# A two-layer encoder trunk on one core: layer 1's attention prepared by key head, its output weights split a piece per step, and the router's sums in one matmul

## The chip, the cores and the metric

The kernel runs on one core of one Trainium2 chip. TensorE (PE) does the matmuls and transposes, VectorE (DVE), ScalarE (ACT) and GpSimd (POOL) the elementwise work, and SyncE (SP) issues the weight loads. The metric is the device time of one execution in microseconds (us), as the median of several runs. All times within an execution count from the start of its span.

## The reference

`reference()` applies two layers to x (512 tokens of 1024 features), all in float32. Each layer is a token mixer and then a mixture of experts, both post-norm and modulated by a conditioning vector:

```
mod = silu(c) @ ada_w[i] + ada_b[i];  sh1, sc1, g1, sh2, sc2, g2 = split(mod, 6)
h = x * (1 + sc1) + sh1
y = neighbourhood_mixer(h) if i == 0 else gqa_mixer(h)
x = layer_norm(ALPHA * x + (1 + g1) * y)
h = x * (1 + sc2) + sh2
y = hierarchical_moe(h)
x = layer_norm(ALPHA * x + (1 + g2) * y)
```

Layer 1's mixer has 16 query heads and 4 key heads of 64 features. Queries and keys are RMS-normalised and rotated (rope), scores are softmaxed over all 512 keys, and the result is multiplied by an output matrix of 1024 x 1024. The router of the experts picks, for each token, the best of 4 groups and the best 2 of its 8 experts, with gates from the two softmaxes. Each of the 32 experts is a gated MLP (1024 to 512 to 1024).

## The kernel before

Tokens lie on the 128 partitions, in 4 tiles t of 128 tokens. Where products need more than one pass's precision, an operand x is split into a rounded part H (ACT copies it to fp32r) and a rest L = x - H (a subtraction), and three matmuls H·H, H·L and L·H are added. `split()` (line 307) does this with the subtraction on POOL unless told otherwise.

The order of PE's instructions is the order of the program text. In layer 0's mixer the DVE keeps that order too, and SP does everywhere. On the other engines, and on the DVE elsewhere, a planner puts the instructions in order when the program is built: the text's order is the priority, and an instruction whose inputs are ready can go ahead of an earlier one that waits. Weights of 1 MB come through a fixed list (`plan`, `W`), each loaded into the next buffer that is free.

Layer 1's mixer is `mixer1` (line 717). It projects keys and values for all tokens (lines 751 to 763), then queries in four parts c, one for each key head (`project(c)`, 96 steps of one matmul). `ahead(c, x)` splits one half of the weights of part c; it is called for part c + 1 at the end of `project(c)`. `rope` rotates a projected tile and sums its squares; `root` makes the RMS factor. `keys(t)` scales the 4 key heads of tile t, splits them, and transposes H and L, each head laid twice side by side (8 transposes of 128 x 128), into kHL. `queries(c, t)` does the like for queries, with H and L side by side (4 transposes). The order is: project(0), then project(1) with keys(t) after each 12 steps, then queries(0, t) after each 12.

The attention then runs over 64 blocks n: part c = n // 16, tile t = n // 4 % 4, query head n % 4. `scores(n + 2)` makes 2 matmuls, a DVE maximum and an ACT exponential; `turn(n)` transposes the result of block n; `finish(u)` weighs the values of four blocks and splits the result (oH, oL; the latter on POOL). Between these, k steps of other PE work are filled in: 8 per block of project(2) and project(3) while c < 2, none for the first 3 blocks of each part and none for n < 36 once c is 2, else 5 steps of the output projection (`halves`, `sums`). At n = 24 `router_weights(1)` (line 389) folds the modulation into the router's weights: 8 matmuls against a broadcast column give a bias, and 8 more against ones give column sums, with a DVE multiplication between. At n = 32 `late()` (line 1099) splits all four 1 MB output weights in one go (`split_wo`, 16 pieces of 128 x 512: ACT copies, POOL subtracts in layer 1), then makes the gain g1 and the scaled norm rows gb by 6 row matmuls (`row`).

`sums(t, h, kh)` is 12 matmuls of the output projection for tile t, half h of the columns and half kh of the rows. For kh = 0 it also scales x by gb and adds to it, on the DVE. 192 steps in all; 125 are filled in before the last block. Then come, between the rest of the steps, `turnX` (transposes of x), `logits` (16 records of router matmuls and the norm's statistics) and `router` for tiles 0 to 2, and `split_z` (a POOL subtraction of 128 x 1024 for each tile).

`moe` (line 1367) is the same in both layers. `begin` gathers the first tokens from tiles 0 to 2 on PE, runs the router of tile 3, marks its slots (`mark`), and gathers tile 3. Then come 8 quarters q of 4 experts: `gate_up`, `turn`, `down`, `combine`. In q = 0 the work filled in behind `gate_up(0)` is gate2(0), gate2(1), the turn, counts, residual(0), residual(1). gate2 is a row matmul and a DVE copy of the second gain; residual(h) is 2 row matmuls and 8 DVE operations of 128 x 512, and holds both buffers `gc` until they are done. `counts` and `turn` share one buffer, `hx`.

## Time and profile before

| | |
|---|---|
| time, median of 3 runs | 1695.33 us (1695.08 to 1695.36) |
| time of the profiled execution | 1693.38 us |
| its span | 1691.6 us |
| mean granted TensorE clock | 0.964 |
| PE busy | 1572.1 us (93%) |
| DVE busy | 718.3 us (42%) |
| ACT busy | 447.8 us (26%) |
| POOL busy | 165.7 us (10%) |
| layer 0, mixer | about 0 to 350 us |
| layer 0, experts | about 360 to 862 us |
| layer 1, mixer | about 862 to 1160 us |
| layer 1, experts | about 1171 to 1665 us |

The profile lists one execution. A share of busy time is a mean over the whole span, so the two expert stages, 0.98 ms of the 1.69 ms, weigh most in it. A row of the timeline gives the start, the length, and behind the brackets how long the engine had been idle and what ended that. PE's rows overlap, since matmuls are pipelined. A granted clock of 1.00 is 2.4 GHz and 0.50 is 1.2 GHz; a value between them is a mean of the two levels over the stretch.

### The profile page before, as it was taken

How to read it: one execution, taken by the hardware profiler on the slowest of the kernel's cores; microseconds unless marked ns; L12 is line 12 of the kernel's file. 1: busy time of each engine (PE TensorE's matmuls, PEld its weight loads, DVE VectorE, ACT ScalarE, POOL GpSimd, SP SyncE). 2: the span in 40 equal slices, each digit the busy share in tenths (PEclk: the TensorE clock that was granted, in tenths of full speed). 3: DMA queues.
4: the chain of work that ended last, by engine and by line, in shares of the span. 5: the costliest groups of instructions: out<-in, count | busy, mean ns of one | idle time of the engine just before them, and what ended most of it. 6: DMA issues, size and time to landing. Idle time of an engine off the chain costs nothing. (4 is left out here: it accounts for less than half of the span.)

```text
span 1691.6 us, 21659 instructions
## 1 busy us (share of the span) xinstructions
PE 1572.1 (93%) x8618; PEld 923.7 (55%) x8618; DVE 718.3 (42%) x1616; ACT 447.8 (26%) x959; POOL 165.7 (10%) x107
## 2 busy tenths in 40 slices
PE   7999997989999999999978896997999999999995
PEld 5676664763445454444468774776354444545442
DVE  3434544664323232231367557667432232323235
ACT  2443334230111111111144655543111111111112
POOL 2322112110000000000032115002000000000001
PEclk9999997999999999999989898997999999999997
DMA  9577873159999999999731000026799999999981
GB/s 336 194 306 282 350 287 135 65 217 381 417 420 418 420 420 418 420 420 418 327 110 51 26 1 0 1 84 264 314 416 419 420 419 418 420 420 419 419 337 51
DMA packets 76199, 493.19 MB, mean 292 GB/s; under 512 B 9876, under 2 KB 11284, under 8 KB 18876
## 3 DMA queue, kind: packets, MB, share of 16 engines
q1 hardware_dynamic: 72636, 485.44, 70.4%
q10 hardware_dynamic: 3456, 6.29, 1.1%
q8 instruction: 70, 1.15, 0.3%
q14 instruction: 37, 0.30, 0.1%
HBM read 489.61 MB, written 2.10 MB: 291 GB/s over the span
## 5 line engine op out<-in xcount | busy, mean ns | idle before, releaser
L299 PE MATMUL gu<-w,xT 128*64 128x512 f32 x2048 | 445.0, 592 | 0.0
L299 PEld LDWEIGHTS gu<-w,xT 128*64 128x64 f32 x2048 | 146.9, 137 | 291.5 <-issue 288.1
L299 PE MATMUL pd<-w,hx 128*64 128x512 f32 x1024 | 227.1, 596 | 0.0
L1479 DVE TENSOR_TENSOR h<-h,gu 128x512 f32<-128x512 f32 x32 | 22.0, 687 | 370.5 <-PE gu L299 370.5
L299 PEld LDWEIGHTS pd<-w,hx 128*64 128x64 f32 x1024 | 70.8, 137 | 138.9 <-issue 135.6
L299 PE MATMUL gc<-OH,zH 128*128 128x256 f32 x480 | 123.5, 294 | 2.0 <-DVE OH L1364 2.0
L299 PE MATMUL gc<-OH,zL 128*128 128x256 f32 x480 | 120.4, 287 | 0.0
L299 PE MATMUL gc<-YH,OT 128*128 128x512 f32 x244 | 104.1, 427 | 1.0 <-DVE X L1446 1.0
L1446 DVE TENSOR_TENSOR X<-X,gc 128x512 f32<-128x512 f32 x128 | 87.2, 687 | 39.5 <-PE gc L299 39.5
L299 PEld LDWEIGHTS gc<-OH,zH 128*128 128x128 f32 x480 | 94.0, 196 | 13.5 <-issue 12.3
L299 PE MATMUL gc<-YL,OT 128*128 128x512 f32 x244 | 96.3, 395 | 0.0
L299 PEld LDWEIGHTS gc<-OH,zL 128*128 128x128 f32 x480 | 94.2, 196 | 0.0
L299 PE MATMUL pj<-w,oH 128*128 128x512 f32 x256 | 87.2, 409 | 0.7 <-DVE g L998 0.7
L1502 ACT ACTIVATE YH<-h 128x512 fp32r<-128x512 f32 x32 | 20.2, 630 | 231.0 <-DVE h L1501 231.0
L1382 ACT ACTIVATE xT<-gc,A 128x256 f32<-128x256 f32 x60 | 33.7, 564 | 175.0 <-PE gc L299 175.0
L299 PE MATMUL pj<-wh,hTH 128*128 128x256 f32 (+1 forms) x240 | 63.4, 312 | 9.4 <-DVE t L776 3.5
L299 PEld LDWEIGHTS gc<-YH,OT 128*128 128x128 f32 x244 | 45.8, 188 | 37.3 <-DVE X L1446 15.8
L1380 DVE TENSOR_SCALAR xT<-gc,A 128x256 f32<-128x256 f32 x60 | 32.5, 543 | 76.9 <-ACT xT L1382 76.5
L1478 ACT ACTIVATE h<-gu 128x512 f32<-128x512 f32 x32 | 19.1, 597 | 173.0 <-PE gu L299 173.0
L302 PE MATMUL pt<-c_ident,pr 128*128 128x128 f32 x384 | 61.6, 286 | 2.8 <-ACT pr L864 1.6
L299 PE MATMUL pj<-wl,hTH 128*128 128x256 f32 (+1 forms) x240 | 60.5, 301 | 2.0 <-POOL wl L312 2.0
L862 DVE TENSOR_REDUCE st<-ps 128x1 f32<-128x512 f32 x64 | 44.0, 689 | 38.5 <-PE ps L299 37.9
(331 smaller groups left out, 2440.2 us busy)
## 6 DMA issues: line engine op xcount, KB each, us to landing
w<-in_gu SPq DMA_DIRECT2D x256, 1024.0 KB, 14.3
w<-in_dn SPq DMA_DIRECT2D x128, 1024.0 KB, 13.9
w<-in_ada SPq DMA_DIRECT2D x40, 1024.0 KB, 7.3
wq<-in_wqk SPq DMA_DIRECT2D x16, 512.0 KB, 3.7
w<-in_wo SPq DMA_DIRECT2D x8, 1024.0 KB, 5.0
w<-in_adaq SPq DMA_DIRECT2D x6, 1024.0 KB, 11.5
bias<-in_nab ACTq DMA_DIRECT2D x24, 256.0 KB, 3.7
w<-in_wq SPq DMA_DIRECT2D x4, 1024.0 KB, 4.8
```

Of the source, the lines that this page charges most:

```text
L299: return self.nc.tensor.matmul(out, l, r, start=start, stop=stop, **kw)
L302: self.nc.tensor.transpose(out, in_, self.ident)
L862: nc.vector.tensor_reduce(s[:, 0:1], ps, axis=AX.X, op=OP.max, negate=True)
L1380: nc.vector.tensor_scalar(xT[q][:, k, :], ps, s, b, op0=OP.mult, op1=OP.add)
L1382: nc.scalar.activation(xT[q][:, k, :], ps, AF.Identity, scale=s, bias=b)
L1446: nc.vector.tensor_tensor(X[t][:, c], X[t][:, c], ps, op=OP.add)
L1478: nc.scalar.activation(h, gu[0], AF.Silu)
L1479: nc.vector.tensor_tensor(h, h, gu[1], op=OP.mult)
L1502: nc.scalar.activation(YH[j][:, c], y, AF.Copy)
```

## The change

- `router_weights`: the DVE makes both products of the router's weights (with the scale and with the shift) and sums each over the 8 row groups; one matmul against ones, 72 columns wide, sums both over the partitions.
- `split_wo` hands out one piece of 128 x 512 per step. In layer 0, `step()` still does 4. In layer 1 the pieces come 2 per block for n = 32 to 35 (kh = 0, subtracted on POOL), and 1 per block for n = 36 to 43 (kh = 1, subtracted on the DVE).
- `ahead`: the weights of parts 0 and 1 are split before project(0) begins, those of part 1 into the tiles PT, which the attention uses later; part 2 is split at the end of project(0), part 3 at the end of project(2).
- `keys(t)` writes each scaled head twice in one DVE operation, transposes that once (4 transposes), and makes H and L from the transposed result.
- project(1) runs 8 steps before keys(0) and 10 after each keys(t).
- Blocks 48 to 50 also get 5 steps each, so 140 steps are done before the last block; the routers of tiles 0 and 1 move into the passes of t = 2 and t = 3.
- The scaling of x by gb goes to POOL for tiles 1 to 3.
- `router` becomes `places`, a generator that stops once the positions are known. In `begin`, gate2(0) stands ahead of it, the mark follows the positions, then the gates, then gate2(1). The fill of q = 0 loses both gate2, so counts and residual(0) stand ahead of the turn.

The diff, without the lines that do not change (each part is headed by the function that it is in):

```diff
@@ router_weights @@
-def router_weights(self, l, pp):
+def router_weights(self, l, pp, pool):
-    ps = pp.tile([P, 36], F32, name="pt")
-    for k in range(KD):
-        self.mm(ps, bcast(A2[:, 1, k:k + 1], [P, P]), wr[:, k, :], k == 0, k == KD - 1)
-    nc.vector.tensor_tensor(rb, ps, self.rb[l], op=OP.add)
+    wb = pool.tile([P, S], F32, name=("dacc", "hf")[l], bufs=3 - l)[:, 0:KD * 36].rearrange("p (k n) -> p k n", k=KD)
+    sm = pool.tile([P, 2, 36], F32, name="wrs")
+    nc.vector.tensor_tensor(wb, wr, bcast(A2[:, 1, :, None], [P, KD, 36]), op=OP.mult)
-    ps = pp.tile([P, 36], F32, name="pt")
-    for k in range(KD):
-        self.mm(ps, bcast(self.Zo[:, 32:33], [P, P]), wr[:, k, :], k == 0, k == KD - 1)
-    nc.scalar.activation(cs, ps, AF.Copy)
+    for n, z in enumerate((wr, wb)):
+        nc.vector.tensor_reduce(sm[:, n, :], z.rearrange("p k n -> p n k"), axis=AX.X, op=OP.add)
+    ps = pp.tile([P, 2, 36], F32, name="pt")
+    self.mm(ps, bcast(self.Zo[:, 32:33], [P, P]), sm, True, True)
+    nc.vector.tensor_tensor(rb, ps[:, 1, :], self.rb[l], op=OP.add)
+    nc.scalar.activation(cs, ps[:, 0, :], AF.Copy)
@@ split_wo @@
-    def step():
-        z = hk.pop(0)
-        x = w[z]
-        wH[z] = pool.tile([P, 2048], F32R, name=f"w{self.nh}")
-        wL[z] = self.W(("wl", l, *z), True)
-        self.free.append(0)
-        for k in range(4):
-            c = slice(512 * k, 512 * k + 512)
-            nc.scalar.activation(wH[z][:, c], x[:, c], AF.Copy)
-            eng = nc.gpsimd if l or k % 2 else nc.vector
-            eng.tensor_tensor(wL[z][:, c], x[:, c], wH[z][:, c].bitcast(F32), op=OP.subtract)
+    def pieces():
+        for z in hk:
+            x = w[z]
+            wH[z] = pool.tile([P, 2048], F32R, name=f"w{self.nh}")
+            wL[z] = self.W(("wl", l, *z), True)
+            self.free.append(0)
+            for k in range(4):
+                c = slice(512 * k, 512 * k + 512)
+                nc.scalar.activation(wH[z][:, c], x[:, c], AF.Copy)
+                eng = nc.gpsimd if (k % 2 if l == 0 else z[1] == 0) else nc.vector
+                eng.tensor_tensor(wL[z][:, c], x[:, c], wH[z][:, c].bitcast(F32), op=OP.subtract)
+                yield
+
+    todo = pieces()
+
+    def step(n=4):
+        for _ in range(n):
+            next(todo, None)
@@ mixer0, neighbours: aside @@
-            self.router_weights(0, pp)
+            self.router_weights(0, pp, pool)
@@ mixer1: ahead @@
-            hl[c].append(self.split(hq, hl[c][0][:, 1024 * x:1024 * x + 1024], [P, 1024], 2))
+            w = hl[c][0][:, 1024 * x:1024 * x + 1024]
+            if c == 1:
+                z = at.tile([P, 2, 1024], F32R, name="PT", bufs=2)
+                nc.scalar.activation(z[:, 0], w, AF.Copy)
+                nc.gpsimd.tensor_tensor(z[:, 1], w, z[:, 0].bitcast(F32), op=OP.subtract)
+                hl[c].append((z[:, 0], z[:, 1]))
+            else:
+                hl[c].append(self.split(hq, w, [P, 1024], 2))
@@ mixer1: project @@
-                    if h is hL and t == NT - 1 and k % 4 == 3:
-                        ahead(c + 1, k // 4)
+                    if h is hL and t == NT - 1 and k % 4 == 3 and c != 1:
+                        ahead(max(2, c + 1), k // 4)
@@ mixer1: keys @@
-        nc.vector.tensor_tensor(kk[t], kk[t], bcast(kr[0][:, t, :, None], [P, 4, HD]), op=OP.mult)
-        kd = [pool.tile([P, S], F32R, name="hf", bufs=2).rearrange("p (h n d) -> p h n d", h=4, n=2) for _ in range(2)]
-        for d in range(2):
-            nc.scalar.activation(kd[0][:, :, d, :], kk[t], AF.Copy)
-        nc.vector.tensor_tensor(kd[1][:, :, 0, :], kk[t], kd[0][:, :, 0, :].bitcast(F32), op=OP.subtract)
-        nc.gpsimd.tensor_tensor(kd[1][:, :, 1, :], kk[t], kd[0][:, :, 1, :].bitcast(F32), op=OP.subtract)
-        for n in range(2):
-            pt = pp.tile([P, 4, P], F32, name="pt")
-            for h in range(4):
-                self.tr(pt[:, h, :], kd[n][:, h].bitcast(F32))
-            if n:
-                nc.vector.tensor_copy(kHL[n][:, :, 128 * t:128 * t + 128], pt)
-            else:
-                nc.scalar.activation(kHL[n][:, :, 128 * t:128 * t + 128], pt, AF.Copy)
+        kd = pool.tile([P, S], F32, name="hf", bufs=2).rearrange("p (h n d) -> p h n d", h=4, n=2)
+        nc.vector.tensor_tensor(kd, bcast(kk[t][:, :, None, :], [P, 4, 2, HD]), bcast(kr[0][:, t, :, None, None], [P, 4, 2, HD]),
+                                op=OP.mult)
+        pt = pp.tile([P, 4, P], F32, name="pt")
+        for h in range(4):
+            self.tr(pt[:, h, :], kd[:, h])
+        H, L = (z[:, :, 128 * t:128 * t + 128] for z in kHL)
+        nc.scalar.activation(H, pt, AF.Copy)
+        nc.vector.tensor_tensor(L, pt, H.bitcast(F32), op=OP.subtract)
@@ mixer1: order before the blocks @@
-    ahead(0, 0)
-    ahead(0, 1)
+    for c in range(2):
+        for x in range(2):
+            ahead(c, x)
+    run(it, 8)
-        run(it, 12)
+        run(it, 10)
@@ mixer1: loop over the 64 blocks @@
-                late()
+                step = late()
-            self.router_weights(1, pp)
-        k = 0 if i < 3 or n < 36 and c > 1 else 8 if c < 2 else 5
+            self.router_weights(1, pp, pool)
+        if 32 <= n < 36:
+            step(2)
+        elif 36 <= n < 44:
+            step(1)
+        k = (0 if i < 3 else 8) if c < 2 else 0 if n < 36 else 5
@@ layer: sums @@
-                nc.vector.tensor_tensor(x, x, gb[:, 0, c], op=OP.mult)
-                nc.vector.tensor_tensor(x, x, gb[:, 1, c], op=OP.add)
+                eng = nc.gpsimd if t else nc.vector
+                eng.tensor_tensor(x, x, gb[:, 0, c], op=OP.mult)
+                eng.tensor_tensor(x, x, gb[:, 1, c], op=OP.add)
@@ layer: late @@
-                for _ in range(4):
-                    step()
@@ layer: late (end) @@
+                return step
@@ layer: order of layer 1's mixer @@
-                    made[0] += 1
-                made = [5 * 28]
-                run(120 + 8 - made[0])
-                run(6)
+                run(4)
-                run(144 - made[0])
-                for t in range(1, NT):
+                for t in range(2, NT):
-                    hx = turnX(t - 1) if t > 1 else None
+                    hx = turnX(t - 1)
-                    if t > 1:
-                        logits(t - 1, lg[:, t - 1, :], hx)
+                    logits(t - 1, lg[:, t - 1, :], hx)
-                    if t != 2:
-                        self.router(t // 2, wk, pp, "pt", lg[:, t // 2, :], rt)
+                    self.router(t - 2, wk, pp, "pt", lg[:, t - 2, :], rt)
+                assert next(it, 0) == 0
@@ router @@
-def router(self, t, pool, pp, tag, lg, rt):
+def router(self, *z):
+    for _ in self.places(*z):
+        pass
+
+def places(self, t, pool, pp, tag, lg, rt):
@@ places (was router), after the position @@
-
+    yield
@@ moe: begin @@
-            self.router(NT - 1, pool, pp, "tp", rt["lg3"], rt)
+            gate2(0)
+            gates = self.places(NT - 1, pool, pp, "tp", rt["lg3"], rt)
+            next(gates)
+            next(gates, None)
+            gate2(1)
@@ moe: fill of the first quarter @@
-                fill = [lambda: gate2(0), lambda: gate2(1), lambda: self.counts(pool, pp, rt),
-                        lambda: residual(0), lambda: residual(1)]
+                fill = [lambda: self.counts(pool, pp, rt), lambda: residual(0), lambda: residual(1)]
```

## Rows read from the trace of the kernel before

**Rows 1.** The page's chain that ended last, by engine (share of the span).

```profile
PE 42%; DVE 5%; ACT 2%; issue 0%; DVEq 0%; ACTq 0%
```

**Rows 2.** Windows: stretch, its length, then busy time of each engine (instructions), granted clock, DMA share, GB/s.

```profile
898.00:932.20 34.20, 30.54 (x241) 29.85 (x241) 26.34 (x78) 14.86 (x35) 9.45 (x8) 0.95 0.17 63
...
932.20:945.00 12.80, 7.06 (x31) 5.11 (x30) 9.17 (x25) 8.08 (x21) 3.81 (x2) 0.69 0.23 82
...
1024.50:1057.00 32.50, 17.73 (x67) 9.31 (x66) 25.19 (x38) 18.44 (x42) 23.69 (x17) 0.79 0.00 1
1062.00:1120.00 58.00, 58.00 (x351) 44.15 (x349) 35.94 (x66) 31.47 (x77) 4.39 (x6) 1.00 0.00 1
1128.00:1170.70 42.70, 32.10 (x188) 26.75 (x187) 33.76 (x126) 15.33 (x37) 8.16 (x4) 0.86 0.78 321
...
1220.00:1640.00 420.00, 420.00 (x2162) 203.43 (x2160) 120.80 (x231) 58.95 (x114) 0.00 (x0) 1.00 1.01 419
```

**Rows 3.** Timeline of layer 1's projections: start, length, engine, line, operation, tiles, [idle before, releaser].

```profile
911.03 4.71 POOL L312 TENSOR_TENSOR wl<-w,wh 128x1024 fp32r<-128x1024 f32 x2 [3.66 <-ACT wh L311]
...
913.77 0.28 PE L299 MATMUL pj<-wh,hTH 128*128 128x256 f32 x1
...
914.85 1.04 PE L302 MATMUL pt<-c_ident,hf 128*128 128x128 f32 x8
...
932.16 0.47 PE L299 MATMUL ps<-kHH,w 128*128 128x512 f32 x1
...
943.14 1.09 PE L302 MATMUL pt<-c_ident,hf 128*128 128x128 f32 x4 [4.10 <-DVE hf L845]
```

**Rows 4.** Lines L291 and L1030 of the DVE: count, shortest, median and longest ns.

```profile
L291 DVE TENSOR_TENSOR rsu<-rsr x5: 174/175/1240, 904.5 to 1038.0; 128x16 f32<-128x16 f32 x5
...
L1030 DVE TENSOR_TENSOR X<-X,gb x8: 675/677/1749, 1034.8 to 1060.5; 128x512 f32<-128x512 f32 x8
```

**Rows 5.** Timeline of the two router_weights, layer 0 first.

```profile
254.65 1.95 PE L299 MATMUL pt<-c_wr,A 128*128 128x36 f32 x16 [0.74 <-DVE A L407]
...
260.54 3.64 PE L299 MATMUL pt<-w,Z 128*32 128x512 f32 x16
...
1000.14 1.87 PE L299 MATMUL pt<-c_wr,A 128*128 128x36 f32 x16
...
1002.16 0.45 DVE L397 TENSOR_TENSOR c_wr<-c_wr,A 128x288 f32<-128x288 f32 x1
1002.75 1.95 PE L299 MATMUL pt<-c_wr,Zo 128*128 128x36 f32 x16 [0.74 <-DVE c_wr L397]
...
1004.53 0.47 PE L299 MATMUL ps<-kHH,w 128*128 128x512 f32 x1
```

**Rows 6.** Timeline of late(), blocks 32 to 36 of layer 1's attention.

```profile
1026.40 7.91 ACT L466 ACTIVATE w<-w 128x512 fp32r<-128x512 f32 x15
...
1027.13 21.92 POOL L468 TENSOR_TENSOR w<-w,w 128x512 fp32r<-128x512 f32 x15 [0.35 <-ACT w L466]
...
1034.85 3.78 PE L299 MATMUL pj<-mod,c_indc 128*128 128x512 f32 x4 [5.55 <-ACT gb L1112]
...
1057.08 0.63 PE L299 MATMUL pj<-w,oH 128*128 128x512 f32 x2
```

**Rows 7.** Timeline of the end of layer 1's mixer.

```profile
1155.51 5.09 POOL L1158 TENSOR_TENSOR zL<-X,zH 128x1024 fp32r<-128x1024 f32 x2 [19.36 <-DVE mod L1032]
...
1170.75 0.56 PE L299 MATMUL gc<-OH,zH 128*128 128x256 f32 x1
```

**Rows 8.** Timeline of the start of layer 1's experts.

```profile
1198.32 1.98 PE L299 MATMUL tp<-mod,c_indc 128*128 128x512 f32 x4
...
1206.13 3.35 PE L299 MATMUL gc<-mod,c_indc 128*128 128x512 f32 x4 [2.98 <-DVE X L1455]
```

**Rows 9.** SP's queue: one batch of weight loads, and issue to landing late in layer 1.

```profile
1216.81 11.10 SPq L271 DMA_DIRECT2D w<-in_gu  x8
...
w<-in_gu SPq DMA_DIRECT2D x16, 1024.0 KB, 18.2
```

## The prediction

> **What bounds the kernel now.** First I read the page's chain: nearly all of it that is listed by engine is PE [rows 1], so a change pays only where PE waits, runs at the low clock, or has less to do. Then the windows [rows 2]. In layer 1's experts (1220 to 1640 us) PE is busy in every microsecond at clock 1.00, and so it is in the second half of the attention (1062 to 1120). Nothing that shifts other engines' work can gain there. Elsewhere there is room: 898 to 932 (projections) has 3.7 us without PE, 932 to 945 (first blocks) 5.7 us and a clock of 0.69, 1024.5 to 1057 (`late` and blocks 32 to 35) 14.8 us and a clock of 0.79, and 1128 to 1170.7 (the mixer's end) 10.6 us and a clock of 0.86. The change works in these four stretches, and in the two `router_weights`, where PE is busy with little matmuls. The sum is made against the profiled execution, 1693.38 us; the median of the three runs is 1.95 us above it.
>
> **Projections and first blocks: -8.** PE stands until 913.77 because project(1) needs the weights that POOL is still subtracting from 911.03 on [rows 3]. The change splits these before project(0), while POOL has little to do, so that wait of about 2.5 us goes. POOL's 4.71 us at the same place remain, now for part 2, which PE needs only 20 us later. keys(t) makes 4 transposes instead of 8: 16 fewer at 1.04 / 8 = 0.13 us, -2. In the projections this makes -4.5. In the first blocks the chain is what counts: from the first scores (932.16) to the first transposes of queries(1) (943.14) are 11.0 us, and POOL's splits for part 2 ran inside it and held DVE operations up (the lock, below). They move 20 us earlier; I take 3.5 off, which leaves 7.5 for a rope, a root of eight small operations and two exponentials. Bounds of the term: -12 (all idle time of both windows and part of the low clock) and -2 (only the transposes, if the four splits at the start hold up the ropes of the keys instead).
>
> **The port that POOL and DVE share.** A DVE operation on 16 columns takes 0.175 us and took 1.24 us while POOL subtracted the output weights; one of 512 columns takes 0.68 and took up to 1.75 [rows 4]. The Trainium skill (SBUF — State Buffer, section "SBUF: two separate sides") calls this an exclusive lock, held for the whole instruction against a DVE operation with two SBUF inputs or in a two-port mode; by it the move of the scaling to POOL is a cost, and rival 1 prices that. The trace agrees (1.24 against 0.175).
>
> **The two `router_weights`: -7.** In layer 1 PE gives it 1000.14 to 1004.53, 4.4 us; in layer 0, with the wait in front, 253.9 to 260.54, 6.6 us [rows 5]. Afterwards PE has one matmul, about 0.3 us. The DVE gets two multiplications of 0.45 us (the row of L397) and two sums of the same 288 columns, taken at 0.45 too: 1.8 us. In layer 1 the planner can bring them forward, since their inputs are long there: -4. In layer 0 the DVE keeps the text's order, so PE waits for them: 0.6 for the fold, 1.8, and 0.3 come to 2.7 of 6.6, -3.9; behind that wait on PE stand the modulation's matmuls (260.54) and the next scores. Then comes a stretch in which ACT, DVE and PE wait for each other in turn, which need not pass all of it on; I take -3. Bounds of the pair: -10 and -2.
>
> **`late` and blocks 32 to 36: -9.** ACT takes the 16 pieces in one go (7.9 us for 15), and the row matmuls wait for ACT's copies of gb until 1034.85; POOL's pieces run to 1049 (21.9 us for 15, 1.46 each) [rows 6]. The first step of the output projection comes at 1057.08, 32.5 us after `late` began, while PE needs about 14 us of it at full clock (17.7 busy at 0.79). With two pieces a block the rows are done about 8 us earlier, and the root of queries(3), which the burst held up, starts as much earlier. If its chain then runs as slowly as now, block 36 starts 8 us earlier; if ACT is the limit (about 17 us of copies, exponentials and pieces) it starts 14 earlier. I take 11. Then 2 go back: blocks 36 to 43 get 8 subtractions of 0.68 us on a DVE that is busy 62% of that stretch (35.9 of 58), partly while POOL still scales x (12 operations at about 1.3 to 1.46). Bounds: -16 (all idle time and the clock) and +2 (rival 1).
>
> **15 steps moved and the mixer's end: -3.5.** Blocks 48 to 50 have no gap on PE [rows 2], so the 15 steps cost about 3.5 there (two matmuls in 0.63 with the tail of the second [rows 6], about 0.23 each). Behind the last block 15 fewer remain, and one of three passes of 24 steps (5.6 us of PE, and what stands between) no longer precedes `logits(1)` and `logits(2)`, so these and the routers that follow them on the DVE come 7 to 8 us sooner. That part is limited by the DVE (33.8 busy of 42.7), and the DVE's work in it hardly shrinks: one of six sums, about 1.4 us. What makes it shorter is that no router waits for its logits any more. I take -7, with the POOL subtractions of 5.09 us still in the way at the end [rows 7]. Bounds: -8 and +3.5 (nothing gained at the end).
>
> **The start of the experts: -1.** The fill behind gate_up(0) loses two row matmuls and two DVE copies; today 1198.32 to 1209.48 passes before `down` [rows 8]. Then counts (some ten small DVE operations, 1.6 us, which now stand ahead because they share `hx` with the turn) and residual(0) take its place: h 0.7, counts 1.6, eight operations of about 0.65, two rows of 0.9, about 9.3 instead of 11.2: -2 in each layer, taking layer 0 like layer 1. In `begin`, the gates leave the path (-0.3), but the row of gate2(0), about 0.9 us, now stands in PE's order between the gathers and the router's matmul, and its DVE copy of about 0.7 can stand ahead of the positions: +1.5 in each layer. Together -1; bounds -4 and +3.
>
> **Sum:** -8 - 7 - 9 - 3.5 - 1 = -28.5 us, 1664.9 for the profiled execution, 1667 as a median.
>
> **Rivals.**
> 1. *POOL keeps the gain of `late`.* The pieces are not spread after all, because ACT may take any piece that is ready, or the 12 scalings get between POOL's 8 pieces, and the first step of the output projection waits for both: 20 x 1.46 = 29 us after 1028 is 1057, where it starts now. For: POOL is then busy without a gap, and the lock is in the trace. Against: the pieces stand first in the text. The term goes from -9 to +2, and the early blocks lose 3: 1681.
> 2. *The clock comes back as well.* The four stretches lose to the low clock 0.05 x 34 + 0.31 x 13 + 0.21 x 32 + 0.14 x 43 = 18 us [rows 2], of which the terms above take about half. If the gaps get short enough, another 9 go: 1658. Against: blocks 32 to 35 still have no fill.
> 3. *The weights arrive too late.* Their loads start when the last scores are done, and the DMA is full (1.01) through the experts [rows 2]. A load is used about 30 us after its issue (12 loads, one item of two experts) and lands after 18.2 at the end [rows 9]: 12 us to spare, of which the shorter end of the mixer takes 7. If the spare is less than I read, up to 7 come back: 1674.
> 4. *Slower than before.* In blocks 32 to 47 every one of the 20 POOL operations (8 pieces, 12 scalings) holds up a DVE operation ahead of a maximum that the next scores need, and PE waits each out in full, at up to 1.75 us [rows 4]: 35 us on top of the forecast, 6.5 above today, about 1702. It decides from 28.5 / 20 = 1.4 us of PE for each POOL operation. Against: today 15 such operations in a row cost PE less than that, since ACT's burst has its part in the gap; the matmuls of scores run two blocks ahead; and DVE operations that read PSUM are not seen to wait.
>
> **How the numbers follow.** Likeliest 0.60, rival 1 0.18, rival 2 0.12, rival 3 0.05, rival 4 0.05. The bounds of the terms, taken as independent (half-widths about 5, 4, 9, 6, 3.5), give 13 us on either side: 1654 to 1680. To take in rival 1 the upper end goes to 1684. What a measurement here can tell from no change is about 0.2%, 3.4 us. Faster by more than that: the likeliest and rivals 1 to 3, less a little for several at their bad ends, 0.93; within it 0.02; slower 0.05.
>
> **What would show it.** In the trace after: no gap on PE between project(0) and project(1); 16 transposes for the keys; one small matmul in each `router_weights`, with PE's wait before it in layer 0 about 2 us; ACT's pieces between exponentials rather than 15 in a row; the first output step some 20 us after `late` begins instead of 32; the stretch from the last block to the gathers 36 rather than 43 us; the experts' length unchanged to 2 us. Wrong would be: POOL busy in one run up to that first step (rival 1), PE with gaps inside 1220 to 1640 (rival 3), or maxima of scores that wait for POOL in blocks 36 to 47 (rival 4).

## The result

The changed kernel takes 1681.14 us (median of three runs, 1680.42 to 1683.32), the kernel before 1695.33: the ratio is 0.992 (95% interval 0.9897 to 0.9942), a gain of 14.2 us. The forecast was 1667, a gain of 28.3. The sign and the range held, the size did not: half of the gain is missing, and the time is the one that rival 1 gave (1681).

The profiled execution of the changed kernel is its slowest, 1683.32 us. In its first 85 us, before any part of the change is reached, it falls 3.6 us behind: the third scores of layer 0 start at 84.73, against 81.13 in the profile of before and 80.88 to 82.62 in the profiles of the fifteen kernels below. PE's first wait, for a load of weights, is 0.9 us longer (7.04 instead of 6.15); what makes up the rest is not shown. So the two traces differ by 10.0 us in span and the medians by 14.2.

### Where the time went, stage by stage

The two traces hold the same PE instructions in nearly the same order, so the start of an instruction after, less its start before, gives a running difference, and the step of it from one landmark to the next is what a stage gained or lost. I worked this table out from the PE timelines (us):

```
up to (PE instruction)                      before    after   running   step  forecast
3rd scores of layer 0                        81.13    84.73     +3.60   +3.6     -
behind router_weights, layer 0              265.52   265.90     +0.38   -3.2    -3
first transposes of layer 1                 871.96   873.49     +1.53   +1.2    -0.5 (experts' start, layer 0)
last transposes of the projections          931.81   931.89     +0.08   -1.5    -4.5
first blocks (to 947)                       947.24   945.41     -1.83   -1.9    -3.5
blocks up to the 8th                        984.47   981.21     -3.26   -1.4     -
behind router_weights, layer 1             1008.56  1000.36     -8.20   -4.9    -4
first step of the output projection        1057.08  1048.99     -8.09   +0.1    -9
logits(0)                                  1130.24  1125.04     -5.20   +2.9    +3.5
first gathers                              1170.75  1159.91    -10.84   -5.6    -7
second item of the experts                 1216.61  1206.57    -10.04   +0.8    -0.5
last matmul                                1671.25  1661.18    -10.07    0.0     0
```

One stage stands out: `late` and blocks 32 to 36, forecast -9, gave nothing. The projections with the first blocks gave 3.4 of 8 (4.8 with the blocks behind). All other stages are within 1.7 us of the forecast.

The page's chain that ended last is, as in [rows 1], nearly all PE; POOL is new in it with 1%:

```profile
PE 41%; DVE 5%; ACT 1%; POOL 1%; issue 1%; ACTq 0%; POOLq 0%; DVEq 0%
```

The windows of the changed kernel that answer to [rows 2], each laid at the same instructions (stretch, length, busy time and count of PE, PEld, DVE, ACT and POOL, granted clock, DMA share, GB/s):

```profile
899.40:932.20 32.80, 28.64 (x223) 27.73 (x224) 26.27 (x74) 11.57 (x26) 8.16 (x4) 0.95 0.26 97
932.20:943.60 11.40, 6.26 (x32) 4.59 (x31) 8.60 (x25) 7.21 (x20) 0.00 (x0) 0.91 0.01 1
1016.40:1049.00 32.60, 16.01 (x67) 9.07 (x66) 26.03 (x36) 16.75 (x40) 28.64 (x21) 0.71 0.00 0
1054.00:1112.00 58.00, 58.00 (x344) 43.96 (x343) 36.73 (x67) 30.35 (x74) 4.39 (x6) 1.00 0.00 1
1123.20:1159.90 36.70, 27.94 (x173) 23.37 (x172) 29.40 (x116) 15.20 (x35) 7.91 (x4) 0.86 0.82 333
1210.00:1630.00 420.00, 420.00 (x2162) 203.36 (x2160) 120.23 (x230) 58.99 (x114) 0.00 (x0) 1.00 1.01 419
```

The third line is the one to read: 32.6 us, as long as before, with PE busy for 16.0 at a clock of 0.71, and POOL busy for 28.6 of 32.6, where it was 23.7 of 32.5. The fifth is the end of the mixer: 36.7 instead of 42.7, as forecast (36). The sixth shows the experts as full as before, so rival 3 (weights too late) did not occur; and in the fourth, 58.00 of 58.00, no maximum of a score holds PE up behind block 36, which rival 4 needed.

The DVE and POOL inside the third line, and what PE waited for (timeline of the changed kernel: start, length, engine, line, operation, tiles, and in brackets the idle time before it and what ended that):

```profile
1016.38 1.02 PE L299 MATMUL pj<-mod,c_indc 128*128 128x512 f32 x2
1018.88 5.88 POOL L469 TENSOR_TENSOR w<-w,w 128x512 fp32r<-128x512 f32 x4 [0.35 <-ACT w L467]
1024.71 2.97 POOL L1047 TENSOR_TENSOR X<-X,gb 128x512 f32<-128x512 f32 x2
1025.23 1.24 DVE L291 TENSOR_TENSOR rsu<-rsr 128x16 f32<-128x16 f32 x1
1026.51 1.20 DVE L292 TENSOR_TENSOR rsu<-rsu,rst 128x16 f32<-128x16 f32 x1
1030.64 1.26 DVE L295 TENSOR_TENSOR rsr<-rsr,rsu 128x16 f32<-128x16 f32 x1
1036.78 1.73 DVE L469 TENSOR_TENSOR w<-w,w 128x512 fp32r<-128x512 f32 x1 [4.88 <-POOL w L469]
1038.44 1.48 DVE L852 TENSOR_TENSOR kk<-kk,rsr 128x256 f32<-128x256 f32 x1
1041.38 1.12 PE L302 MATMUL pt<-c_ident,hf 128*128 128x128 f32 x4 [11.28 <-DVE hf L855]
1047.25 1.09 PE L302 MATMUL pt<-c_ident,hf 128*128 128x128 f32 x4 [3.04 <-DVE rz L896]
1048.99 1.05 PE L299 MATMUL pj<-w,oH 128*128 128x512 f32 x2
```

The first row matmul of `late` and the first transposes of `queries(3)` in the kernel before:

```profile
1024.64 1.02 PE L299 MATMUL pj<-mod,c_indc 128*128 128x512 f32 x2
1054.11 0.60 PE L302 MATMUL pt<-c_ident,hf 128*128 128x128 f32 x4
```

Against [rows 6], the pieces are spread and the rows no longer wait behind ACT's burst. But the scalings (L1047) start on POOL at 1024.71, in the middle of its 8 pieces. The root of `queries(3)` (L291 to L295) still pays 1.2 us for three of its four operations on 16 columns; the first of the later pieces, now on the DVE, stands ahead of the products with the root (L852) and waits 4.88 us for POOL; and the first of these products takes 1.48. PE waits 11.28 us for that chain. Its first transposes of `queries(3)` come at 1041.38, 25.0 us after the first row matmul of `late`, where it was 29.5 before: 4.5 us are gained up to there. They are lost again right behind it. The next two products (2.91 us) and another later piece (1.75) stand on the DVE ahead of the second tile, PE waits 3.04 us more for its transposes at 1047.25, and the first step of the output projection follows only then.

### The profile page after: what moved, and what is told of

Same layout as the page of the kernel before. It is cut to its first block, busy times and chain, and to the rows that moved or that the text cites. A ratio compares the mean times of both kernels' runs of the same rounds, so it can differ in the third digit from the quotient of the medians.

```text
span 1681.6 us, 21494 instructions
## 1 busy us (share of the span) xinstructions
PE 1558.6 (93%) x8542; PEld 911.8 (54%) x8542; DVE 719.9 (43%) x1614; ACT 445.6 (26%) x951; POOL 168.5 (10%) x107
## 3 DMA queue, kind: packets, MB, share of 16 engines
q8 instruction: 70, 1.15, 0.3%
## 5 line engine op out<-in xcount | busy, mean ns | idle before, releaser
L1395 DVE TENSOR_SCALAR xT<-gc,A 128x256 f32<-128x256 f32 x60 | 32.5, 544 | 74.7 <-ACT xT L1397 74.3
L299 PE MATMUL pj<-wh,hTH 128*128 128x256 f32 (+1 forms) x208 | 53.4, 312 | 9.7 <-DVE t L784 3.5
L1506 ACT ACTIVATE hx<-tp 128x512 f32<-128x512 f32 x32 | 19.0, 594 | 149.3 <-PE tp L302 129.0
L872 DVE TENSOR_REDUCE st<-ps 128x1 f32<-128x512 f32 x64 | 44.0, 689 | 33.5 <-PE ps L299 33.1
## 6 DMA issues: line engine op xcount, KB each, us to landing
w<-in_gu SPq DMA_DIRECT2D x256, 1024.0 KB, 14.6
```

The costliest lines, as they stand in the source:

```text
L299: return self.nc.tensor.matmul(out, l, r, start=start, stop=stop, **kw)
L872: nc.vector.tensor_reduce(s[:, 0:1], ps, axis=AX.X, op=OP.max, negate=True)
L1395: nc.vector.tensor_scalar(xT[q][:, k, :], ps, s, b, op0=OP.mult, op1=OP.add)
L1506: nc.scalar.activation(hx, pt, AF.Copy)
```

## The experiments

Three theories were stated for `late`. Theory 1: what counts is the new wait, the 4.88 us for POOL in front of the products. Theory 2: what counts is POOL's activity as such, which stretches the DVE's operations in the chain of `queries(3)`. Theory 3: that chain is as long in any case. "L" below is the time from the first row matmul of `late` to the first step of the output projection, read from the PE timelines: 32.4 us before, 32.6 after.

**Scalings back on the DVE.**

```diff
-                    eng = nc.gpsimd if t else nc.vector
+                    eng = nc.vector
```

> The changed kernel with the 12 scalings of the residual back on the DVE; the 8 early pieces stay on POOL, the 8 later ones on the DVE. Theory 1 (the DVE's first later piece stands ahead of the key products of queries(3) and waits 4.9 us for POOL's last early piece, which the scalings had delayed): POOL's 8 pieces run in one go and end about 11 us after the first, the DVE's wait goes, the first output step comes 6 to 8 us sooner; 12 x 0.68 = 8 us more on the DVE give 2 to 3 back: 1675. Theory 2 (no particular wait; POOL's operations slow the DVE's by the shared port): POOL has 12 operations fewer, also about 1675. Theory 3 (the stretch is bounded by the chain of queries(3) itself): 1681 to 1683.

Measured 1668.47 us (1668.19 to 1668.76), ratio to before 0.9845 (0.9828 to 0.9863): 12.7 faster than the changed kernel, twice what theories 1 and 2 said, and theory 3 falls. L is 22.2 us, and `logits(0)` comes 97.6 us after the first row matmul instead of 108.7, so nearly the whole gain is made here. POOL has only its 8 pieces left, and PE waits 4.92 us for the chain instead of 11.28:

```profile
1012.82 1.02 PE L299 MATMUL pj<-mod,c_indc 128*128 128x512 f32 x2
1015.33 11.10 POOL L469 TENSOR_TENSOR w<-w,w 128x512 fp32r<-128x512 f32 x7 [0.35 <-ACT w L467]
1030.84 1.12 PE L302 MATMUL pt<-c_ident,hf 128*128 128x128 f32 x4 [4.92 <-DVE hf L855]
1035.00 0.63 PE L299 MATMUL pj<-w,oH 128*128 128x512 f32 x2
```

**All pieces on POOL, still spread.**

```diff
-                    eng = nc.gpsimd if (k % 2 if l == 0 else z[1] == 0) else nc.vector
+                    eng = nc.gpsimd if l or k % 2 else nc.vector
```

> The changed kernel with all 16 pieces subtracted on POOL, still spread over the blocks; scalings stay on POOL. Theory 1 (the wait of the DVE for POOL): no piece is on the DVE, so that wait of 4.9 us cannot occur, though POOL has 28 operations in a row (about 37 us); the later pieces are needed only some 19 blocks on: 1675 to 1677. Theory 2 (POOL's activity slows the DVE): 8 more POOL operations, 1684. Theory 3: 1681.

Measured 1676.59 (1674.95 to 1678.85), ratio 0.989 (0.9871 to 0.9908); L 28.3. As theory 1 said, 4.5 us are gained: with no piece on the DVE there is no wait of the DVE for one. The 8 subtractions have left the DVE as well, so the run does not give the wait a price of its own. But 8 us more were to be had, so it is not the whole.

**Engines of the pieces exchanged.**

```diff
-                    eng = nc.gpsimd if (k % 2 if l == 0 else z[1] == 0) else nc.vector
+                    eng = nc.gpsimd if (k % 2 if l == 0 else z[1]) else nc.vector
```

> The changed kernel with the engines of the pieces exchanged: the 8 early pieces on the DVE, the 8 later ones on POOL; scalings stay on POOL. Theory 1: nothing on the DVE waits for POOL's pieces and the first output step waits for DVE pieces alone; the first output step 17 to 20 us after the rows of late instead of 33: 1671 to 1674. Theory 2: POOL has as many operations as now in the same stretch, 1680 to 1682. Theory 3: 1681.

Measured 1681.1 (1679.59 to 1684.2), ratio 0.9922 (0.9901 to 0.9944): no gain, L 32.6. My theory 1 had promised 7 to 10 us here, and it falls as the sole cause. In the trace of this kernel the DVE does not wait for POOL in front of the products, and yet they start at 1038.34, 22.8 us after the first row matmul (22.1 in the changed kernel):

```profile
1029.49 10.05 POOL L1048 TENSOR_TENSOR X<-X,gb 128x512 f32<-128x512 f32 x6
...
1032.12 0.67 DVE L872 TENSOR_REDUCE st<-ps 128x1 f32<-128x512 f32 x1
...
1033.08 1.23 DVE L292 TENSOR_TENSOR rsu<-rsu,rst 128x16 f32<-128x16 f32 x1
1034.23 0.68 DVE L1048 TENSOR_TENSOR X<-X,gb 128x512 f32<-128x512 f32 x1
1034.84 1.23 DVE L293 TENSOR_SCALAR rsu<-rsu 128x16 f32<-128x16 f32 x1
1035.99 0.68 DVE L1047 TENSOR_TENSOR X<-X,gb 128x512 f32<-128x512 f32 x1
1036.59 1.23 DVE L295 TENSOR_TENSOR rsr<-rsr,rsu 128x16 f32<-128x16 f32 x1
1037.74 0.68 DVE L1048 TENSOR_TENSOR X<-X,gb 128x512 f32<-128x512 f32 x1
1038.34 4.29 DVE L852 TENSOR_TENSOR kk<-kk,rsr 128x256 f32<-128x256 f32 x3
```

While POOL goes through six operations of 10.05 / 6 = 1.68 us, from 1033.08 on every second operation of the DVE takes 1.23 us, though on 16 columns, and the pair (1.23 and 0.68, overlapping a little) starts anew every 1.75 us, about once for each of POOL's. The maximum that reads PSUM (L872) keeps its 0.67. The exchange has a second effect, which I had not counted: the 8 early pieces now stand on the DVE ahead of the root and take 9.5 us there. What POOL's activity costs is therefore read against the run with everything on the DVE, below.

**Rows and scalings moved to block 36.**

```diff
+                    def rows():
+                        for n in range(2):
...
-                    return step
+                    return step, rows
...
+            if n == 36:
+                rows()
```

> The changed kernel with the four row matmuls and copies of gb moved from late to block 36, so that no scaling is ready before; engines as in the changed kernel. Theory 1: POOL's 8 early pieces run in one go as soon as ACT delivers them, the DVE's first later piece no longer waits: the first output step 8 us sooner, 1673 to 1675. Theory 2: the 20 POOL operations remain and fall into a stretch in which the DVE is busier: 1681 or more. Theory 3: 1681.

Measured 1677.08 (1676.61 to 1677.41), ratio 0.9895 (0.9877 to 0.9913). L is 22.0, 10.6 less than in the changed kernel, so the chain was freed as theory 1 said. But 6.4 of them are lost again up to `logits(0)` (104.4 us after the first row matmul, 108.7 in the changed kernel). Behind the first step POOL now has the scalings while the DVE has the later pieces (1.12 us each instead of 0.68), and PE waits twice:

```profile
1043.98 1.12 PE L302 MATMUL pt<-c_ident,pr 128*128 128x128 f32 x4 [3.45 <-ACT PT L884]
1049.01 0.44 PE L302 MATMUL pt<-c_ident,rze 128*128 128x128 f32 x2 [2.21 <-ACT w L859]
```

```profile
1034.90 8.24 POOL L1049 TENSOR_TENSOR X<-X,gb 128x512 f32<-128x512 f32 x5 [7.71 <-ACT gb L1131]
1043.10 8.43 POOL L1050 TENSOR_TENSOR X<-X,gb 128x512 f32<-128x512 f32 x5
```

Theory 1 was right on the first half, theory 2 on the second: at either place the scalings on POOL cost time.

**Work on POOL that nobody needs.**

```diff
+                    for n in range(2 if t else 0):
+                        nc.gpsimd.tensor_tensor(spare, gb[:, 0, c], gb[:, 1, c], op=OP.add)
```

added to the kernel with the scalings on the DVE.

> The kernel with the scalings back on the DVE (1668.5), with 12 further additions of 128x512 on POOL at the places where the scalings stood, into a tile that nothing reads before the end of the mixer. Theory 2 (POOL's activity as such stretches the DVE's operations with two SBUF inputs, and with them the chain of queries(3)): the gain of that kernel goes, 1676 to 1682, and the 16-column operations of the root take over 1 us again while POOL runs. Theory 1 (a wait for a result of POOL made the difference): nothing waits for the added operations, 1668 to 1670.

Measured 1683.03 (1681.07 to 1684.78), ratio 0.9926 (0.9909 to 0.9942), L 32.9: the whole gain is gone. Nothing waits for a result of the added operations, and yet they cost 14.6 us. They do so in both ways: three of them stand between POOL's pieces, and the DVE's first later piece waits 2.44 us for the last of these pieces; and behind it the root and the products are stretched:

```profile
1035.58 1.74 DVE L469 TENSOR_TENSOR w<-w,w 128x512 fp32r<-128x512 f32 x1 [2.44 <-POOL w L469]
1037.24 1.23 DVE L295 TENSOR_TENSOR rsr<-rsr,rsu 128x16 f32<-128x16 f32 x1
...
1040.59 2.29 DVE L852 TENSOR_TENSOR kk<-kk,rsr 128x256 f32<-128x256 f32 x2
```

**Everything on the DVE.** All 16 pieces there as well, on top of the scalings.

```diff
+                    eng = nc.gpsimd if l == 0 and k % 2 else nc.vector
```

> All 16 pieces and all scalings on the DVE; POOL has no part in late. Theory 2: no operation of the DVE is stretched, but 8 x 0.66 = 5.3 us of pieces come onto the DVE ahead of the chain of queries(3), about what the stretching by the 8 POOL pieces costs now (11 us at up to twice the duration): 1667 to 1670. Theory 1: the first output step waits for the DVE alone, 1666. If the DVE is the bound there: 1673 or more.

Measured 1669.07 (1668.42 to 1669.83), ratio 0.9849 (0.9832 to 0.9865), L 20.6: as fast as with 8 pieces on POOL. What those 8 pieces take off the DVE and what they cost it are equal here. Against the kernel with the engines exchanged this run shows the stretching by itself. Both have the 8 early pieces on the DVE, and in neither does the DVE wait for POOL from `late` to the first step. The exchanged kernel has 20 operations on POOL that stand on the DVE here, and it takes 12.0 us more (1681.1 against 1669.07): the early pieces take 9.5 us of the DVE there and 5.2 here, and L is 32.6 against 20.6. The groups of the DVE between 1010 and 1062 (busy time, mean ns of one, idle before) for the last step of the root and the products, first in the changed kernel, then with the scalings on the DVE, then with everything on it:

```profile
L852 DVE TENSOR_TENSOR kk<-kk,rsr 128x256 f32<-128x256 f32 x4 | 4.8, 1218 | 0.0
L295 DVE TENSOR_TENSOR rsr<-rsr,rsu 128x16 f32<-128x16 f32 x1 | 1.3, 1261 | 0.0
```

```profile
L852 DVE TENSOR_TENSOR kk<-kk,rsr 128x256 f32<-128x256 f32 x4 | 1.8, 477 | 0.0
L295 DVE TENSOR_TENSOR rsr<-rsr,rsu 128x16 f32<-128x16 f32 x1 | 0.2, 163 | 0.0
```

```profile
L852 DVE TENSOR_TENSOR kk<-kk,rsr 128x256 f32<-128x256 f32 x4 | 1.5, 410 | 0.0
L295 DVE TENSOR_TENSOR rsr<-rsr,rsu 128x16 f32<-128x16 f32 x1 | 0.2, 161 | 0.0
```

**The spreading alone**, on the kernel before: the hunks of the pieces, `late` and the loop, not those of the scalings or the order.

> The kernel before with one part alone: the 16 pieces issued over blocks 32 to 43, the 8 later ones on the DVE; the scalings stay on the DVE as before. Theory 2 (it was the scalings on POOL that took the gain of the spread pieces away): the prediction's term of -9 is there, 1684 to 1687. If spreading the pieces is worth nothing by itself: 1693 to 1696.

Measured 1683.55 (1681.77 to 1686.18) against 1695.12, ratio 0.9929 (0.9912 to 0.9945): -11.6, and L 22.0. The forecast of this part, -9 with a first step "some 20 us after `late` begins", was good; what undid it was the move of the scalings.

**The two `router_weights` alone**, on the kernel before.

> The kernel before with one part alone: the two router_weights with one matmul each. By the prediction's term -7: 1688. By the trace of the changed kernel 3.3 in layer 0 and 4.2 in layer 1: 1687 to 1688. If the stretch behind it in layer 0 passes nothing on: 1690 to 1691.

Measured 1686.9 (1682.4 to 1687.93), ratio 0.9947 (0.9926 to 0.9967): -8.2, forecast -7. In the changed kernel PE's wait in layer 0 is 3.0 us (forecast about 2, since a sum over the 288 columns takes 0.66 and not 0.45), and layer 1 has none:

```profile
260.89 0.41 PE L299 MATMUL pt<-wrs,Zo 128*128 128x72 f32 x2 [3.00 <-DVE wrs L398]
...
997.71 0.34 PE L299 MATMUL pt<-wrs,Zo 128*128 128x72 f32 x2
```

**Keys and splits alone**, on the kernel before.

> The kernel before with one part alone: keys doubled and transposed once, and the splits of part 1 ahead of project(0). By the prediction's term -8: 1686 to 1687. By the trace of the changed kernel (3.4 us from 898 to the second block, and 1.4 up to the 4th, since POOL's splits now fall on the ropes of the keys): 1690 to 1692.

Measured 1690.9 (1689.02 to 1695.0) against 1694.91, ratio 0.9977 (0.9967 to 0.9987): -4.0, half of the forecast. Two runs looked for the other half. Both start from the kernel with the scalings on the DVE (1668.5).

**Four subtractions left out**, and in a second run moved to the DVE.

```diff
-                    nc.gpsimd.tensor_tensor(z[:, 1], w, z[:, 0].bitcast(F32), op=OP.subtract)
-                    hl[c].append((z[:, 0], z[:, 1]))
+                    hl[c].append((z[:, 0], z[:, 0][:, 0:1024]))
...
```

> The kernel with the scalings on the DVE (1668.5), with the four POOL subtractions for the weights of parts 1 and 2 in layer 1 left out: the product of the low part is computed with the high part instead, with as many matmuls. Theory 2 (these splits, moved onto the ropes of the keys, stretch them and so kept half of the projections' term): 2 to 4 us faster, 1664.5 to 1666.5, no DVE operation over 1 us in the projections. If the wait of PE there comes from the chain of the root and the ropes itself: 1668 to 1669.

> The kernel with the scalings on the DVE (1668.5), with the same four subtractions on the DVE (1024 columns, estimated 1.3 us each from 0.68 for 512) instead of POOL. Theory 2: the stretching goes (about 4 us of DVE time), but 5.2 us come onto the DVE, which is busy 26 of 33 us there: 1667 to 1670.

Measured 1669.15 (1668.81 to 1669.56) without them and 1668.79 (1667.27 to 1670.34) with them on the DVE; ratios 0.9853 and 0.9849, both the same as 0.9845. Here the 2 to 4 us of theory 2 are not found: POOL's splits do stretch a rope (1.68 us at 916.29 in the changed kernel, where 0.42 is usual), but with them gone PE still waits at two of three places. The longest waits of PE in this stretch, in the kernel before, then in the changed kernel (with the scalings on the DVE they are the same to 0.1), and then without the subtractions:

```profile
913.43 0.39 PE L299 MATMUL pj<-wl,hTH 128*128 128x256 f32 x1 [2.04 <-POOL wl L312]
921.14 0.63 PE L302 MATMUL pt<-c_ident,hf 128*128 128x128 f32 x4 [0.91 <-DVE rsu L293]
926.20 0.63 PE L302 MATMUL pt<-c_ident,hf 128*128 128x128 f32 x4 [0.70 <-DVE hf L845]
```

```profile
918.73 0.63 PE L302 MATMUL pt<-c_ident,hf 128*128 128x128 f32 x4 [1.41 <-DVE hf L838]
921.91 0.63 PE L302 MATMUL pt<-c_ident,hf 128*128 128x128 f32 x4 [1.41 <-DVE vrs L792]
925.97 0.63 PE L302 MATMUL pt<-c_ident,hf 128*128 128x128 f32 x4 [0.84 <-DVE hf L855]
```

```profile
916.91 0.63 PE L302 MATMUL pt<-c_ident,hf 128*128 128x128 f32 x4 [1.41 <-DVE vrs L792]
920.97 0.63 PE L302 MATMUL pt<-c_ident,hf 128*128 128x128 f32 x4 [0.92 <-DVE hf L859]
```

One of three waits goes. Counted from the same matmul at the start of the stretch (894.94 with the scalings on the DVE, 896.22 here), the PE timelines of the two kernels put its worth at 1.8 us at the end of the keys and 2.7 in the first blocks, and at block 8 1.15 of it are left (977.67 and 977.80). That is one execution of each; the measured times, 1668.47 and 1669.15, show nothing of it.

**Moved steps and the mixer's end alone**, on the kernel before.

> The kernel before with one part alone: 15 steps moved into blocks 48 to 50 and the new order of the mixer's end. By the prediction's term -3.5, and by the trace of the changed kernel +3.3 and -5.6: 1691.5 to 1693. If the DVE is the bound at the end: 1695 to 1698.

Measured 1691.81 (1690.19 to 1695.17) against 1694.17, ratio 0.9985 (0.9976 to 0.9995): -2.4, forecast -3.5.

**Gate rows back in the fill**, on the kernel with the scalings on the DVE.

> The kernel with the scalings on the DVE (1668.5), and the two gate rows back where they were, in the fill of the first quarter of the experts, the routing in one piece. By the traces (the stretch from the gathers to the second item is 1.2 us longer than before in layer 0 and 0.8 in layer 1) it gains 2: 1666.5. By the prediction (the new place saves 0.5 in each layer) it loses 1: 1669.5.

Measured 1669.41 (1667.13 to 1671.75) against 1668.47 of that kernel in another set of runs; ratio to before 0.9846 (0.9828 to 0.9865) against 0.9845: no difference that these runs can tell. The step of +1.2 us in layer 0's experts, which I had read from the traces as a loss, is not the edit's: from the first gathers to those of the second item the kernel with the keys alone, whose code there is that of before, takes 60.45 us, the kernel before 57.80 and the changed one 59.15.

**Two tries for a faster kernel.** Rows at block 36 together with the scalings on the DVE, and the same with all pieces on the DVE.

> The kernel with the scalings on the DVE (1668.5), with the four row matmuls and the copies of gb moved to block 36, so that the scalings come behind the chain of queries(3) and not ahead of it. Theory 2: the 4 scalings that stand ahead of the root (6 us of the DVE, partly stretched by POOL's pieces) go out of the chain, and the row matmuls leave the stretch where PE waits: 1662 to 1666. Against it: they fall into blocks 36 to 47, where the DVE is busier: 1668 to 1670.

> As the run with rows at block 36 and scalings on the DVE, and all 16 pieces on the DVE too, so that POOL has no part in late. Theory 2: no stretched operation, and ahead of the chain stand 8 pieces (5.3 us) instead of scalings: 1663 to 1668; better than the run with 8 pieces on POOL only if their stretching costs more than 5.3 us.

Measured 1669.35 (1667.67 to 1670.37) and 1670.69 (1669.3 to 1672.86), ratios 0.9845 and 0.9861. Neither beats 1668.5. L is 22.0 in the first, no shorter than with the scalings ahead of the root: without them the first transposes of `queries(3)` come 14.0 us after the first row instead of 18.0, but the rows themselves then take 4.2 us of PE before the first step (1032.38 to 1036.90 in its timeline). So the best version of those measured is the changed kernel with one word of it undone, the scalings on the DVE: 1668.5, 12.7 below the changed kernel and 26 below the one before.

## Why the prediction failed

The edits alone add up: -4.0 (keys) - 8.2 (`router_weights`) - 11.6 (spreading) - 2.4 (order) and 0 (gates) are -26.2 us, and the kernel with all of them but the moved scalings is 26.3 below before. Each of the four has an interval of 1.6 to 3.5 us on either side, about 5 for the sum, so agreement to 0.1 is luck. The forecast sum was -28.5, inside that interval. What the sum lacked is the price of one edit: the 12 scalings on POOL cost 12.7 us.

- *Late and blocks 32 to 36, -9: this step failed.* It had two parts. That the rows are done earlier and that a first step can come 20 us after `late` begins was right (L 22.0 alone). Wrong was the term for POOL: "Then 2 go back", with the scalings placed beside blocks 36 to 43. I had read in [rows 4] what POOL does to the DVE, 1.24 us for an operation of 0.175, but charged it only to the subtractions of blocks 36 to 43. The planner does not keep the scalings for when they are needed: gb is ready by 1024, so they go between POOL's pieces, and POOL works almost without a gap through the whole root and the products of `queries(3)`, which are the chain that sets block 36. The burst of pieces that held this chain up before was merely replaced by another of POOL.
- *Rival 1* named the place, the time and what would show it (POOL busy in one run up to the first step), and was given 0.18. Its mechanism was only partly right: it let the first step wait for all 20 POOL operations. In the exchanged kernel the first step waits for none of POOL's pieces, and comes no sooner. What it waits for is the DVE's chain, which POOL stretches and, in the changed kernel, holds up once for 4.88 us. That the time came out at rival 1's 1681 is in part luck: it took 11 us off the term of `late` and 3 off the early blocks, while in the trace `late` fell short by 9.1 and the projections and first blocks by 4.6, the latter for another reason.
- *Projections and first blocks, -8: mis-sized, -4.0.* The wait for POOL's split went, and 16 transposes with it, as said, so that -2 and -2.5 were expected in the projections (the wait ended at 913.43, not 913.77, and was 2.04 us). But PE then waits for the DVE's products and root instead, 3.66 us in the three rows of the changed kernel above, where before it waited 0.91 and 0.70. I had not looked at what was late next there: the new product over 512 columns (0.68, L838) stands between the ropes on a DVE that is busy 26 of 33 us. That this order is the cause is read from the rows; no run tested it. My lower bound blamed POOL's early splits for such a result; without those of parts 1 and 2 the measured time is the same, and the trace leaves them 1.15 of the missing 4 us. In the first blocks I had taken 3.5 off the 11.0 us between the first scores and the first transposes of queries(1), for DVE operations that POOL held up. The trace of before has one such operation there (L779, 1.13 us instead of 0.42), and with POOL idle the changed kernel still takes 9.5 (932.25 to 941.72).
- *The two `router_weights`, -7: -8.2.* Right, in place and mechanism; the wait in layer 0 is 3.0 us instead of about 2.
- *15 steps moved and the mixer's end, -3.5: -2.4 alone.* In the trace +2.9 and -5.6 for +3.5 and -7.
- *Start of the experts, -1: nothing that can be told.*
- *Rivals 2 to 4* did not decide the time: the clock in the four stretches is 0.95, 0.91, 0.71 and 0.86, against 0.95, 0.69, 0.79 and 0.86 in [rows 2], so it came back in the first blocks alone; the experts have no gap; behind block 36 PE waits for no maximum.

The Trainium skill (SBUF — State Buffer, section "SBUF: two separate sides") lets whichever of the two engines starts first hold the shared port for its whole instruction, if the DVE's has two SBUF inputs or runs in a two-port mode. The trace agrees: 1.23 us for 16 columns while POOL's operation lasts 1.68, and 0.67 for a maximum from PSUM at the same time. The Trainium skill (Perfetto Trace Analysis, section "Optimizing Scalar/DVE Operations") warns that moving work between the DVE and GpSimd might not help for this reason; here it cost 12.7 us.

## What to carry to other kernels

Before moving work from the DVE to POOL because POOL is idle, list which DVE operations with SBUF inputs run meanwhile: if a chain of small dependent ones is among them, each can wait out one of POOL's operations, however short it is itself (here the steps of a root, the products behind it, and a wait for a piece that the moved work delayed: 12.7 us in all). Ask when the moved work becomes ready, not when it is needed, since a planner issues it as soon as it can, between the work that was meant to go first. And where a wait on one engine is removed, read which engine is the next to be late before the wait is booked as gain.

## What the runs showed of the hardware that was not expected

- POOL is slowed as well: an operation of 128x512 takes 1.26 us at its shortest and 1.68 in the mean while the DVE has operations of its own in between (10.05 / 6 in the kernel with the engines exchanged).
- Operations with one SBUF input are hit too: L293, an operation with two constants on 16 columns, took 1.23 us, and a copy of 256 columns 1.36 instead of 0.28 (L898 in the kernel with the added operations).
- Subtractions that are worth 8 x 0.66 = 5.3 us of the DVE cost the same on either engine: 1668.5 with them on POOL, 1669.1 on the DVE.
